# Im2col on one core: eight channels per partition and three uneven loads

## The chip, the cores and the metric

The kernel runs on one core of a Trainium2 chip. The metric is the device time of that core in microseconds (us); the time before is the median of three runs. One execution was also taken by the hardware profiler. Its span, from the first to the last instruction, is shorter than the time, because the time also holds what lies around the instructions. The engines named here are VectorE (DVE in the profile) and ScalarE (ACT), which copy; SyncE (SP), which issues the transfers; and the 16 DMA engines, which move data between the chip's main memory (HBM) and the on-chip memory of 128 partitions.

## The reference

The input `x` has the shape (16, 64, 32, 32) in float32, and `kernel_size` is 3. For each image and channel, the reference lays the 3 x 3 patches around all 30 x 30 positions side by side:

```python
cols = np.zeros((batch, c * kernel_size * kernel_size, h_out * w_out), dtype=np.float32)
for b in range(batch):
    col_idx = 0
    for i in range(h_out):
        for j in range(w_out):
            patch = x[b, :, i:i + kernel_size, j:j + kernel_size].copy()
            cols[b, :, col_idx] = patch.ravel()
            col_idx += 1
```

Read by output row, this is a plain copy: row (channel, ki, kj) of an image is the 30 x 30 window of that channel which starts at (ki, kj). Nothing is computed. One channel of 1,024 numbers (4,096 bytes) becomes nine windows of 900 numbers (32,400 bytes). In all 4.19 MB are read and 33.18 MB are written.

## The kernel before

Each partition holds two neighbouring channels (`CPP` = 2), so the 1,024 pairs of image and channel make four groups of 128 partitions. All four loads are issued first, each into a tile of its own. Then each group is copied window by window, in turn by ScalarE and VectorE, into one of two output tiles. The first group is stored one channel at a time, the other three whole.

```python
x_v = x.rearrange("b (cp c2) h w -> (b cp) c2 (h w)", c2=CPP)
out_v = out.rearrange("b (cp c2 kk) n -> (b cp) c2 (kk n)", c2=CPP, kk=KK)

in_pool = ctx.enter_context(tc.tile_pool(name="in_pool", bufs=n_groups))
out_pool = ctx.enter_context(tc.tile_pool(name="out_pool", bufs=2))

in_tiles = []
for g in range(n_groups):
    row0 = g * P
    in_tile = in_pool.tile([P, CPP, H, W], x.dtype, name="in_tile")
    nc.sync.dma_start(                                   # the loads
        out=in_tile,
        in_=x_v[row0 : row0 + P].rearrange("r c2 (h w) -> r c2 h w", h=H),
    )
    in_tiles.append(in_tile)

for g in range(n_groups):
    # ... row0, in_tile of this group
    out_tile = out_pool.tile([P, CPP, KK, HO, WO], x.dtype)
    ncopy = 0
    for c2 in range(CPP):
        for kk in range(KK):
            # ... src: the window in in_tile; dst: out_tile[:, c2, kk]
            if ncopy % 2 == 0:
                nc.scalar.copy(out=dst, in_=src)
            else:
                nc.vector.tensor_copy(out=dst, in_=src)
            ncopy += 1
        if g == 0:
            nc.sync.dma_start(                           # one channel
                out=out_v[row0 : row0 + P, c2],
                in_=out_tile[:, c2].rearrange("p kk i j -> p (kk i j)"),
            )
    if g != 0:
        nc.sync.dma_start(                               # two channels
            out=out_v[row0 : row0 + P].rearrange("r c2 n -> r (c2 n)"),
            in_=out_tile.rearrange("p c2 kk i j -> p (c2 kk i j)"),
        )
```

Of the kernel before, what the change touches and what calls it, by code (L numbers as in the profile page):

```python
# [1 line left out]

# [4 lines left out]


def _im2col_fast(ctx, tc, x, K, out, CPP):  # L10
    nc = tc.nc
    P = nc.NUM_PARTITIONS

    B, C, H, W = x.shape
    HO = H - K + 1
    WO = W - K + 1
    KK = K * K

    ROWS = B * C // CPP
    n_groups = ROWS // P  # L20

    x_v = x.rearrange("b (cp c2) h w -> (b cp) c2 (h w)", c2=CPP)
    out_v = out.rearrange("b (cp c2 kk) n -> (b cp) c2 (kk n)", c2=CPP, kk=KK)

    in_pool = ctx.enter_context(tc.tile_pool(name="in_pool", bufs=n_groups))
    out_pool = ctx.enter_context(tc.tile_pool(name="out_pool", bufs=2))

    in_tiles = []
    for g in range(n_groups):
        row0 = g * P  # L30
        in_tile = in_pool.tile([P, CPP, H, W], x.dtype, name="in_tile")
        nc.sync.dma_start(
            out=in_tile,
            in_=x_v[row0 : row0 + P].rearrange("r c2 (h w) -> r c2 h w", h=H),
        )
        in_tiles.append(in_tile)

    for g in range(n_groups):
        row0 = g * P
        in_tile = in_tiles[g]  # L40
        out_tile = out_pool.tile([P, CPP, KK, HO, WO], x.dtype)

        ncopy = 0
        for c2 in range(CPP):
            for kk in range(KK):
                ki, kj = divmod(kk, K)
                src = in_tile[:, c2, ki : ki + HO, kj : kj + WO]
                dst = out_tile[:, c2, kk]
                if ncopy % 2 == 0:
                    nc.scalar.copy(out=dst, in_=src)  # L50
                else:
                    nc.vector.tensor_copy(out=dst, in_=src)  # L52
                ncopy += 1

            if g == 0:
                nc.sync.dma_start(
                    out=out_v[row0 : row0 + P, c2],
                    in_=out_tile[:, c2].rearrange("p kk i j -> p (kk i j)"),
                )

        if g != 0:
            nc.sync.dma_start(
                out=out_v[row0 : row0 + P].rearrange("r c2 n -> r (c2 n)"),
                in_=out_tile.rearrange("p c2 kk i j -> p (c2 kk i j)"),
            )


def _im2col_generic(ctx, tc, x, K, out):
    nc = tc.nc
    P = nc.NUM_PARTITIONS  # L70

    B, C, H, W = x.shape
    HO = H - K + 1
    WO = W - K + 1
    KK = K * K

    x_rows = x.rearrange("b c h w -> (b c) (h w)")
    out_rows = out.rearrange("b ck n -> (b ck) n").rearrange(
        "(bc kk) n -> bc (kk n)", kk=KK
    )  # L80

    n_rows = B * C
    n_groups = (n_rows + P - 1) // P

    in_pool = ctx.enter_context(tc.tile_pool(name="in_pool", bufs=min(n_groups, 4)))
    out_pool = ctx.enter_context(tc.tile_pool(name="out_pool", bufs=2))

    for g in range(n_groups):
        row0 = g * P
        nrows = min(P, n_rows - row0)  # L90

        in_tile = in_pool.tile([P, H, W], x.dtype, name="in_tile_g")
        nc.sync.dma_start(
            out=in_tile[:nrows],
            in_=x_rows[row0 : row0 + nrows].rearrange("r (h w) -> r h w", h=H),
        )

        out_tile = out_pool.tile([P, KK, HO, WO], x.dtype, name="out_tile_g")
        for kk in range(KK):
            ki, kj = divmod(kk, K)  # L100
            src = in_tile[:nrows, ki : ki + HO, kj : kj + WO]
            dst = out_tile[:nrows, kk]
            if kk % 2 == 0:
                nc.scalar.copy(out=dst, in_=src)
            else:
                nc.vector.tensor_copy(out=dst, in_=src)

        nc.sync.dma_start(
            out=out_rows[row0 : row0 + nrows],
            in_=out_tile[:nrows].rearrange("p kk i j -> p (kk i j)"),  # L110
        )


@with_exitstack
def kernel(
    ctx: ExitStack,
    tc: tile.TileContext,
    x: bass.AP,
    kernel_size: bass.AP,
    out: bass.AP,  # L120
):
    nc = tc.nc
    P = nc.NUM_PARTITIONS

    K = int(kernel_size)
    B, C, H, W = x.shape
    HO = H - K + 1
    WO = W - K + 1
    KK = K * K
    assert out.shape == (B, C * K * K, HO * WO)  # L130

    dt_size = mybir.dt.size(x.dtype)

    CPP = 0
    for cand in (2, 1):
        if C % cand:
            continue
        rows = B * C // cand
        if rows % P:
            continue  # L140
        free_bytes = cand * KK * HO * WO * dt_size
        if free_bytes >= 2**16:
            continue
        n_groups = rows // P
        sbuf_need = 2 * free_bytes + n_groups * cand * H * W * dt_size
        if sbuf_need > 190 * 1024:
            continue
        CPP = cand
        break

    if CPP:
        _im2col_fast(ctx, tc, x, K, out, CPP)
    else:
        _im2col_generic(ctx, tc, x, K, out)


# [1 line left out]
_INS = ['x', 'kernel_size']  # L158
_OUTS = [((16, 576, 900), 'float32')]
#: Inputs that are plain numbers.  # L160
_NUMBERS = {'kernel_size': 3}


# [26 lines left out]
```

## Time and profile before

| | before |
|---|---|
| time, median of 3 runs | 92.78 us (92.61 to 93.19) |
| span of the profiled execution | 91.3 us |
| VectorE busy | 19.6 us, 36 copies, 623 ns each |
| ScalarE busy | 32.0 us, 36 copies, 938 ns each, and one table load |
| read from and written to HBM | 4.19 MB and 33.18 MB |

A copy's duration is longer than the step to the next copy on the same engine, since consecutive copies overlap a little; where the prediction adds up copies, it takes the step. The profile's page also gives the busy share of each engine and of the DMA in 40 equal slices of the span, each some 2.3 us, as digits in tenths. The span holds nine transfers of data: four loads and five stores, all issued by SyncE on one queue.

### The profile page before, as it was taken

The numbers are of one execution on the slowest core, as the hardware profiler recorded it, in microseconds if no ns is written. First come the engines' busy times: TensorE is split into PE (matmuls) and PEld (weight loads), VectorE is DVE, ScalarE is ACT, GpSimd is POOL, SyncE is SP. The second block draws the span as 40 slices with busy tenths as digits, with TensorE's granted clock in tenths as the row PEclk, the third lists the DMA queues.
The fourth block names the chain that finished last, engine by engine and source line by source line (L and its number), as shares of the span: only waits on it lengthen the run. The fifth ranks groups of instructions, "written<-read, shape, count | busy, mean of one in ns | idle before, by whom it ended". The sixth has DMA issues, their size and how long they took to land.

```text
span 91.3 us, 141 instructions
## 1 busy us (share of the span) xinstructions
DVE 19.6 (22%) x36; ACT 32.0 (35%) x37; POOL 0.2 (0%) x4
## 2 busy tenths in 40 slices
DVE  0059997000000049600000199000000000000000
ACT  5059999991000049980000199920000000000000
POOL 0000000000000000000000000000000000000000
DMA  2899999999999999899999999999999999999960
GB/s 36 373 406 431 427 463 426 412 440 440 426 426 440 554 454 398 369 426 398 454 454 454 454 454 454 454 454 454 454 454 426 426 398 398 426 426 426 426 284 0
DMA packets 1297, 37.37 MB, mean 409 GB/s; under 512 B 145, under 2 KB 145, under 8 KB 145
## 3 DMA queue, kind: packets, MB, share of 16 engines
q1 hardware_dynamic: 1296, 37.37, 95.7%
q14 instruction: 1, 0.00, 0.0%
HBM read 4.19 MB, written 33.18 MB: 409 GB/s over the span
## 4 chain that ended last, share of the span: by engine, by line
DMA 40%; ACT 24%; ACTq 1%; issue 0%
DMA out_dram<-out_tile 34%; ACT out_tile L50 24%; DMA in_tile<-in_x_dram 5%; ACTq L185 1%; ACTq L50 0%
## 5 line engine op out<-in xcount | busy, mean ns | idle before, releaser
L50 ACT COPY out_tile<-in_tile 128x900 f32<-128x900 f32 x36 | 30.7, 938 | 27.2 <-DMA out_dram<-out_tile 23.6
L52 DVE COPY out_tile<-in_tile 128x900 f32<-128x900 f32 x36 | 19.6, 623 | 37.6 <-DMA out_dram<-out_tile 31.9
L50 ACT ACT_TABLE_LOAD x1 | 1.3, 1283 | 0.7 <-PEq L171 0.7
L171 POOL MEMSET const-bfloat16-1.0<- 128x1 bf16 x1 | 0.1, 102 | 0.0
L171 POOL MEMSET const-uint8-127<- 128x1 uint8 x1 | 0.1, 102 | 0.0
L171 POOL MEMSET const-float32-0.0<- 128x1 f32 x1 | 0.1, 99 | 0.2 <-issue 0.2
L171 POOL MEMSET const-float32-1.0<- 128x1 f32 x1 | 0.1, 99 | 0.0
## 6 DMA issues: line engine op xcount, KB each, us to landing
out_dram<-out_tile SPq DMA_DIRECT2D x3, 8100.0 KB, 30.5
out_dram<-out_tile SPq DMA_DIRECT2D x2, 4050.0 KB, 16.6
in_tile<-in_x_dram SPq DMA_DIRECT2D x4, 1024.0 KB, 7.9
```

The lines of the kernel that those rows point to most:

```text
L50: nc.scalar.copy(out=dst, in_=src)
L52: nc.vector.tensor_copy(out=dst, in_=src)
L171: nc = _bacc.Bacc("TRN2", target_bir_lowering=False, num_devices=1)
L185: with _tile.TileContext(nc) as tc:
```

## The change

Each partition now holds eight neighbouring channels, so that the 1,024 pairs of image and channel fill the 128 partitions once. There is one input tile, which stays for the whole kernel, and it is filled by three loads: rows 0 to 31 of the partition's 256 rows (channel 0, 4 KB per partition), rows 32 to 239 (26 KB), rows 240 to 255 (2 KB). The channels are then copied in pairs into two output tiles that take turns as before. The first pair is stored one channel at a time, the other three pairs together. Of each five copies VectorE takes three and ScalarE two. The aim is to start copying after a small first load, to have few and long transfers after it, and to give the faster copy engine more of the copies. The generic path for other shapes and the choice of `CPP` are gone.

```diff
+    CPP = B * C // P
-    x_v = x.rearrange("b (cp c2) h w -> (b cp) c2 (h w)", c2=CPP)
+    x_v = x.rearrange("b (cp c2) h w -> (b cp) (c2 h w)", c2=CPP)
     out_v = out.rearrange("b (cp c2 kk) n -> (b cp) c2 (kk n)", c2=CPP, kk=KK)
-    in_pool = ctx.enter_context(tc.tile_pool(name="in_pool", bufs=n_groups))
+    in_pool = ctx.enter_context(tc.tile_pool(name="in_pool", bufs=1))
     out_pool = ctx.enter_context(tc.tile_pool(name="out_pool", bufs=2))
-    (the loop over four loads, each into a tile of its own)
+    in_tile = in_pool.tile([P, CPP, H, W], x.dtype, name="in_tile")
+    in_flat = in_tile.rearrange("p c h w -> p (c h w)")
+    cuts = [0, H, CPP * H - H // 2, CPP * H]
+    for r0, r1 in zip(cuts, cuts[1:]):
+        nc.sync.dma_start(
+            out=in_flat[:, r0 * W : r1 * W], in_=x_v[:, r0 * W : r1 * W]
+        )
+    on_act = (False, True, False, True, False)
+    n = 0
+    for c in range(0, CPP, 2):
+        out_tile = out_pool.tile([P, 2, KK, HO, WO], x.dtype, name="out_tile")
+        for s in range(2):
             for kk in range(KK):
                 ki, kj = divmod(kk, K)
-                src = in_tile[:, c2, ki : ki + HO, kj : kj + WO]
-                dst = out_tile[:, c2, kk]
-                if ncopy % 2 == 0:
+                src = in_tile[:, c + s, ki : ki + HO, kj : kj + WO]
+                dst = out_tile[:, s, kk]
+                if on_act[n % len(on_act)]:
                     nc.scalar.copy(out=dst, in_=src)
                 else:
                     nc.vector.tensor_copy(out=dst, in_=src)
-            if g == 0:
+            if c == 0:
                 nc.sync.dma_start(
-                    out=out_v[row0 : row0 + P, c2],
+                    out=out_v[:, s],
                     (from that half of out_tile, as before)
-        if g != 0:
+        if c > 0:
             nc.sync.dma_start(
-                out=out_v[row0 : row0 + P].rearrange("r c2 n -> r (c2 n)"),
+                out=out_v[:, c : c + 2].rearrange("p c n -> p (c n)"),
                 (from the whole out_tile, as before)
```

More of the change, by code (lines that the diff above doesn't have):

```diff
@@ L5, with _im2col @@
 import concourse.tile as tile
-from concourse import bass_utils, mybir
-from concourse._compat import with_exitstack
-def _im2col_fast(ctx, tc, x, K, out, CPP):
+from concourse import mybir
+def _im2col(ctx, tc, x, K, out):
     nc = tc.nc
@@ L17, in _im2col_fast @@
     KK = K * K
-    ROWS = B * C // CPP
-    n_groups = ROWS // P
-    x_v = x.rearrange("b (cp c2) h w -> (b cp) c2 (h w)", c2=CPP)
+    assert out.shape == (B, C * KK, HO * WO)
+    CPP = B * C // P
+    assert CPP * P == B * C and C % CPP == 0 and CPP % 4 == 0
+    x_v = x.rearrange("b (cp c2) h w -> (b cp) (c2 h w)", c2=CPP)
     out_v = out.rearrange("b (cp c2 kk) n -> (b cp) c2 (kk n)", c2=CPP, kk=KK)
-    in_pool = ctx.enter_context(tc.tile_pool(name="in_pool", bufs=n_groups))
+    in_pool = ctx.enter_context(tc.tile_pool(name="in_pool", bufs=1))
     out_pool = ctx.enter_context(tc.tile_pool(name="out_pool", bufs=2))
[L28 to L31, printed above, removed]
+    in_tile = in_pool.tile([P, CPP, H, W], x.dtype, name="in_tile")
+    in_flat = in_tile.rearrange("p c h w -> p (c h w)")
+    cuts = [0, H, CPP * H - H // 2, CPP * H]
+    for r0, r1 in zip(cuts, cuts[1:]):
         nc.sync.dma_start(
-            out=in_tile,
-            in_=x_v[row0 : row0 + P].rearrange("r c2 (h w) -> r c2 h w", h=H),
-        )
[L36 to L44, printed above, removed]
+            out=in_flat[:, r0 * W : r1 * W], in_=x_v[:, r0 * W : r1 * W]
+        )
+    on_act = (False, True, False, True, False)
[3 more added lines that the diff above has]
+        for s in range(2):
             for kk in range(KK):
                 ki, kj = divmod(kk, K)
-                src = in_tile[:, c2, ki : ki + HO, kj : kj + WO]
-                dst = out_tile[:, c2, kk]
-                if ncopy % 2 == 0:
+                src = in_tile[:, c + s, ki : ki + HO, kj : kj + WO]
+                dst = out_tile[:, s, kk]
+                if on_act[n % len(on_act)]:
                     nc.scalar.copy(out=dst, in_=src)
@@ L52, in _im2col_fast @@
                     nc.vector.tensor_copy(out=dst, in_=src)
-                ncopy += 1
-            if g == 0:
+                n += 1
+            if c == 0:
                 nc.sync.dma_start(
-                    out=out_v[row0 : row0 + P, c2],
-                    in_=out_tile[:, c2].rearrange("p kk i j -> p (kk i j)"),
+                    out=out_v[:, s],
+                    in_=out_tile[:, s].rearrange("p kk i j -> p (kk i j)"),
                 )
-        if g != 0:
+        if c > 0:
             nc.sync.dma_start(
-                out=out_v[row0 : row0 + P].rearrange("r c2 n -> r (c2 n)"),
-                in_=out_tile.rearrange("p c2 kk i j -> p (c2 kk i j)"),
-            )
[L68 to L114, printed above, removed]
+                out=out_v[:, c : c + 2].rearrange("p c n -> p (c n)"),
+                in_=out_tile.rearrange("p c kk i j -> p (c kk i j)"),
+            )
 def kernel(
-    ctx: ExitStack,
     tc: tile.TileContext,
@@ L121 @@
 ):
[L122 to L154, printed above, removed]
+    with ExitStack() as ctx:
+        _im2col(ctx, tc, x, int(kernel_size), out)
 _INS = ['x', 'kernel_size']
```

## The prediction, made before the changed kernel ran

> **What bounds the kernel now.** I read the page's busy row and slice rows first, because the two copy engines are so idle that something else must set the end:
>
> ```profile
> DVE 19.6 (22%) x36; ACT 32.0 (35%) x37; POOL 0.2 (0%) x4
> ...
> DMA  2899999999999999899999999999999999999960
> GB/s 36 373 406 431 427 463 426 412 440 440 426 426 440 554 454 398 369 426 398 454 454 454 454 454 454 454 454 454 454 454 426 426 398 398 426 426 426 426 284 0
> ...
> q1 hardware_dynamic: 1296, 37.37, 95.7%
> ```
>
> VectorE works for 22% of the span, ScalarE for 35%; the 16 DMA engines are full from the second slice (2.3 us) to the 38th (86.7 us), and the packets of the one data queue take 95.7% of 16 engines' span. There is no slice in between in which the DMA waits for a copy. A slice's rate jumps (369 to 554) because a packet of 64,800 bytes lasts as long as a slice; so I asked for longer stretches. Columns: stretch and length, busy time and count of each engine, PE clock, DMA share, GB/s:
>
> ```profile
> 3.00:11.00 8.00, 5.39 (x11) 5.39 (x7) 0.00 (x0) 1.00 1.01 426
> 14.00:30.00 16.00, 1.38 (x3) 6.89 (x9) 0.00 (x0) 1.00 1.00 433
> 33.10:52.13 19.03, 4.93 (x9) 7.69 (x9) 0.00 (x0) 1.00 1.01 436
> 52.13:71.10 18.97, 4.93 (x9) 7.69 (x9) 0.00 (x0) 1.00 1.01 437
> ```
>
> Loads run at 426 GB/s, one-channel stores at 433, two-channel stores at 436 and 437, with a DMA share of 1.0 in all four: the engines are full, and at nearly one rate in either direction.
>
> Then the DMA issues (count, size of each, median us from issue to landing) and the chain of waits in order of time:
>
> ```profile
> out_dram<-out_tile SPq DMA_DIRECT2D x3, 8100.0 KB, 30.5
> out_dram<-out_tile SPq DMA_DIRECT2D x2, 4050.0 KB, 16.6
> in_tile<-in_x_dram SPq DMA_DIRECT2D x4, 1024.0 KB, 7.9
> ```
> ```profile
> 0.73 4.85 DMA in_tile<-in_x_dram
> ...
> 20.92 31.21 DMA out_dram<-out_tile
> ...
> 52.23 0.95 ACT out_tile L50
> ```
>
> Asked one by one, the nine DMAs land in the order of their issue. The first load lands at 5.6, the fourth at 13.7 (11.6 after its issue at 2.1). The stores, issued at 10.0, 13.3, 20.9, 40.8 and 60.0, land at 23.4, 33.0, 52.1, 71.3 and 90.4. The gaps are 9.6 and 19.1 us, which are sizes and not waits. The chain's 24% of ScalarE is misleading: it goes back from the last store to the copies before it, although that store was issued at 60.0 and stood behind the fourth until 71.3. The 5 us chain piece at the start is real.
>
> The packet records close the account. There is one packet per partition and DMA, eight partitions per engine: 8,192 bytes take 309 ns, 32,400 take 1,200, 64,800 take 2,391 (medians). The last two give 27.2 bytes/ns and some 9 ns fixed per packet; 8,192 / 27.2 + 9 = 310 fits the first. Per engine: 4 x 8 x 309 + 2 x 8 x 1,200 + 3 x 8 x 2,391 ns = 9.9 + 19.2 + 57.4 = 86.5 us. The span is 91.3, so only 4.8 us are not packet time: 1.8 before the first packet starts, 0.9 after the last landing at 90.4, and about 2.1 of first-read delay, completion and unevenness of the engines. Of the last I can place one part: the fourth load's sixteen completions spread over 12.6 to 13.8, against 10.2 to 10.6 for the third, and some load packets between 11.2 and 12.9 take 320 to 650 ns instead of 309, where the first store's packets follow in the same rings. The slowest engine loses about 0.75 us there (13.75 instead of 10.55 + 2.47 = 13.0) and keeps that loss to the end.
>
> **What the Trainium skill says.** All from its page "DMA: Bandwidth & Descriptors". The section "Where 436 GB/s comes from" puts the fabric's ceiling at 435 GB/s; the trace agrees with 436 to 437 in the long stores. "Queues, rings and completion order" says that each DMA engine takes descriptors of a ring in order; the landings in order of issue fit. "Why small descriptors are slow (HBM only)" names a fixed overhead per packet; here it is some 9 ns. "Latency and other measured facts" has copies with a row pitch of 512 KiB at 207 GB/s against 214 in full, and at half of that only from 4 MiB. The new loads have a pitch of 32 KiB, far below, and the new stores one of 259,200 bytes, no power of two. No run here shows those pitches yet.
>
> **The change part by part.**
>
> Bytes: none added or removed. Stores are still two of one channel and three of two channels, with the same 32,400 and 64,800 bytes contiguous per partition: 76.6 us of packets per engine, unchanged.
>
> Loads: four packets of 8,192 per partition become 4,096, 26,624 and 2,048. By the fitted line these are 159, 987 and 84 ns; times 8 partitions 1.27 + 7.90 + 0.67 = 9.84 us against 9.89. Gain: 0.05 us. One issue on SyncE less (425 ns median), but the first starts the stream at the same 0.73, so nothing.
>
> The first wait: the first load is half as large, so it lands 8 x (309 - 159) = 1.2 us earlier, at about 4.4. Channel 0 is now 5 copies on VectorE (a start every 538 ns in the trace) and 4 on ScalarE (844 ns): 3 x 0.844 + 0.94 = 3.5 us. The first store is issued at about 7.9 rather than 10.0. That puts it in the rings earlier, but behind loads that run until about 12.4. Worth nothing by itself.
>
> What has to be tested is whether every later store is still issued before the one ahead of it has drained. Reckon about 1.0 us from issue to first packet (0.73 to 1.75 for the first load).
> - Store 1: issue 7.9, ready 8.9; loads drain 12.3. Slack 3.4.
> - Store 2: channel 1 must now wait for the 26 KB load, landing at 4.4 + 7.9 = 12.3, or 13 if the late loss falls on it. 6 copies on VectorE, 3 on ScalarE: 6 x 0.538 = 3.3. Issue 16.3, ready 17.3; store 1 drains at about 21.9. Slack 4.6.
> - Store 3: 18 copies, 11 on VectorE (5.9) and 7 on ScalarE (5.9). Issue 22.3, ready 23.3; store 2 drains at 31.5. Slack 8.
> - Store 4: its buffer comes free when store 2 lands, 33.0; 10 on VectorE, 8 on ScalarE, 6.8 us. Issue 39.9; store 3 drains at 50.6. Slack 10.
> - Store 5: buffer free at 52.1; 5.9 to 6.0 us. Issue 58.2; store 4 drains at 69.8. Slack 11.
>
> The new split of the copies (43 on VectorE, 29 on ScalarE, from 36 and 36) takes ScalarE's 7.7 us per tile to about 6: all of it beside transfers. So no store is late, and the sum is 92.78 - 0.05, within the scatter of the three runs (92.61 to 93.19).
>
> **The rivals.**
>
> 1. The first copies wait for all three loads, if the one input tile is released as a whole rather than by region. Then they start at about 13.4, store 1 is issued at 17 and its packets begin at 18, while the DMA has drained at 12.3: 5.7 us more, 98.5. Against it: separate cuts would have no sense then. For it: the kernel before, with four input tiles, shows no case. Chance 4%.
>
> 2. The strided layout slows the transfers. All stores and the large load now step over eight channels per partition instead of two. Before, the two one-channel stores already stepped (32,400 bytes at a pitch of 64,800) and ran at 433. A loss of 2% needs 1.9 us, over 2% of all packet time or 19% of load time. Chance 5%.
>
> 3. The turn from loads to stores goes differently. The 0.75 us lost there may vanish, since a small load ends the stream and the store stands ready 3.4 us ahead (some 92.0), or grow as much (93.5) because more store packets are ready beside small ones. Plausible either way, and both under 1%; this sets the width of my range.
>
> 4. A real gain over 2% would need transfers above 437 GB/s or fewer bytes. With 86.4 us of packets, 1.8 ahead and 0.9 behind, and 0.8 because the first packets last 1.04 to 1.25 us instead of 0.31, the floor of the span is 89.9 for sixteen even engines; with the 1.5 by which the time exceeds the span, 91.4. Chance 3%.
>
> **Range and chances.** I take 92.6: minus 0.05 for packets and minus a little for the turn. The range 92.0 to 93.4 holds the turn's gain below, and its loss and the scatter above. Faster by over 2% (under 90.9) 3%, within 2% 91%, slower by over 2% (over 94.6) 6%, which is most of rivals 1 and 2.
>
> **What would show it.** Right, if DMA is full from slice 2 to 38 again, the first store is issued near 8 and the second near 16, the five stores land 9.6 or 19.1 us apart with the last near 90.3, and ScalarE falls to about 28.5 us busy, VectorE rises to 27. Wrong, if copies start at 13 instead of 4.4 (rival 1), if a 64,800-byte store takes over 19.5 us between landings or the loads land after 14.5 (rival 2), or if an empty slice stands between two stores.

## The result and the profile after

The changed kernel takes 93.47 us (median of 4 runs, 93.40 to 93.60) against 92.69 us of the kernel before in its 4 runs: a ratio of 1.0077, with an interval of 1.0048 to 1.0106. (The ratios in this document are estimates with 95% intervals; they can differ a little from the quotient of the two medians, 1.0084 here.) It is slower by 0.8%, a difference that its runs show clearly. The time lies just above the range of the prediction (92.0 to 93.4), and within the 2% to which the prediction gave 91%. All later runs of the kernel before have a median span of 91.0 us and a time 1.8 us above it; the profile of before shown above (91.3) was one of its longer executions. The changed kernel's span is 91.7 in the profile.

The page of the changed kernel, first the engines' busy time, then the DMA's share in 40 slices and its rate, then the data queue:

```profile
DVE 23.5 (26%) x43; ACT 26.2 (29%) x30; POOL 0.2 (0%) x4
...
DMA  3999979999999999999999999999989799997990
GB/s 39 434 442 430 372 298 438 396 438 453 453 424 396 438 453 452 452 452 452 452 452 452 453 452 452 452 452 452 452 368 424 339 396 452 452 424 339 424 452 0
...
q1 hardware_dynamic: 1152, 37.37, 96.4%
```

As before, the DMA engines are the full ones and nothing waits for a copy: no slice before the last is empty. But the fifth and sixth slices (9.2 to 13.8 us), with the digits 9 and 7, move 372 and 298 GB/s, the least of the first half after the start.

In time, with the SyncE rows showing when transfers were issued (start, length, engine, line, what, how many):

```profile
4.58 3.48 ACT L49 COPY out_tile<-in_tile 128x900 f32<-128x900 f32 x4 [2.56 <-DMA in_tile<-in_x_dram]
4.58 2.78 DVE L51 COPY out_tile<-in_tile 128x900 f32<-128x900 f32 x5 [4.58 <-DMA in_tile<-in_x_dram]
8.08 9.09 SPq L54 DMA_DIRECT2D out_dram<-out_tile  x2
13.43 8.54 ACT L49 COPY out_tile<-in_tile 128x900 f32<-128x900 f32 x10 [5.38 <-DMA in_tile<-in_x_dram]
13.43 9.23 DVE L51 COPY out_tile<-in_tile 128x900 f32<-128x900 f32 x17 [6.08 <-DMA in_tile<-in_x_dram]
```

The copies do start at 4.6 and the first store is issued at 8.1, as predicted. Between 8.1 and 13.4 no copy runs at all; the engines wait for the 26 KB load, which was to land at 12.3 and lands at 13.4. The issues (count, size, median us to landing) have it too:

```profile
in_tile<-in_x_dram SPq DMA_DIRECT2D x1, 3328.0 KB, 12.2
in_tile<-in_x_dram SPq DMA_DIRECT2D x1, 512.0 KB, 3.8
in_tile<-in_x_dram SPq DMA_DIRECT2D x1, 256.0 KB, 12.4
```

Issued at 1.16 and 1.64, the last two land at 13.4 and 14.1. From there all is as before: the stores land at 23.8, 33.4, 52.6, 71.7 and 90.8, with gaps of 9.6 and three times 19.1. Against the profile of before (23.4 to 90.4) the whole difference of 0.4 us is there when the first store lands, and stays. (The medians differ by 0.8 us, more than the two profiles, because the profiled execution of before was 0.3 us longer than its median span.)

The place can be narrowed. The first line is the window from 10.5 to 13.5 us of the kernel before, the second the same window of the changed one (columns as in the prediction; the last two are DMA share and GB/s):

```profile
10.50:13.50 3.00, 3.00 (x7) 3.00 (x5) 0.00 (x0) 1.00 1.08 427
```
```profile
10.50:13.50 3.00, 0.07 (x1) 0.07 (x1) 0.00 (x0) 1.00 1.00 306
```

The share is full in both, the rate falls from 427 to 306 GB/s: the packets last longer. (A window counts a packet whole where it starts, so that a share can exceed 1; the rate over the share is 395 against 306.) In the packet records, the last 26 KB packet of each of the 16 engines, all begun between 10.7 and 11.1, takes 1.24 to 2.17 us, 1.68 on average, where 0.99 is the median. To compare kernels with loads of different sizes I use one number, the **stretch**: for all load packets on the loads' queue that end after 10.4 us, the duration less what the fitted line of the prediction gives for their size, summed and divided by 16 engines. It is 0.24 us for the kernel before and 0.89 us for the changed one. Each value of it, here and below, comes from the one profiled execution of that kernel.

### The profile page after: what moved, and what is told of

Same layout as the page of the kernel before. It is cut to its first block, busy times and chain, and to the rows that moved or that the text cites. A ratio compares the mean times of both kernels' runs of the same rounds, so it can differ in the third digit from the quotient of the medians.

```text
span 91.7 us, 138 instructions
## 1 busy us (share of the span) xinstructions
DVE 23.5 (26%) x43; ACT 26.2 (29%) x30; POOL 0.2 (0%) x4
## 4 chain that ended last, share of the span: by engine, by line
DMA 46%; DVE 16%; DVEq 1%; SPq 0%; issue 0%
DMA out_dram<-out_tile 33%; DVE out_tile L51 16%; DMA in_tile<-in_x_dram 13%; DVEq L102 1%; SPq L34 0%; DVEq L51 0%; SPq L59 0%
## 5 line engine op out<-in xcount | busy, mean ns | idle before, releaser
L49 ACT COPY out_tile<-in_tile 128x900 f32<-128x900 f32 x29 | 24.9, 940 | 31.8 <-DMA out_dram<-out_tile 23.8
L51 DVE COPY out_tile<-in_tile 128x900 f32<-128x900 f32 x43 | 23.5, 624 | 35.2 <-DMA out_dram<-out_tile 24.5
## 6 DMA issues: line engine op xcount, KB each, us to landing
in_tile<-in_x_dram SPq DMA_DIRECT2D x1, 256.0 KB, 12.4
```

## The experiments

Four theories fit this profile. **P**: the long packets are at fault; at the turn from loads to stores every engine has one of 26 KB in hand. **Q**: reading eight channels per partition, 32 KB apart, is slow. **T**: the short 2 KB packets are at fault. **S**: a store that is issued earlier and stands waiting while the loads still run stretches them. Times are medians of 4 to 22 runs, with one exception that is named, and ratios are to runs of the kernel before on the same chip.

### Other cuts of the loads, same layout

```diff
-    cuts = [0, H, CPP * H - H // 2, CPP * H]
+    cuts = [0, 2 * H, 4 * H, 6 * H, 8 * H]           # four even loads
+    cuts = [0, H, CPP * H]                           # two loads, 4 and 28 KB
+    cuts = [c * H for c in range(CPP + 1)]           # eight loads
```

Four even loads:

> Edit: the changed kernel with four loads of 8 KB per partition instead of 4, 26 and 2 KB. Theory P (the loss sits in the long load packets: the last 26 KB packet of every DMA engine lasted 1.68 us on average instead of 0.99): the loads end as in the kernel before, slowest completion of the last near 13.7 instead of 14.09, last store lands near 90.4 instead of 90.84, ratio to before 0.997 to 1.003. Theory Q (the loads read eight channels per partition, 32 KB apart, and that is slow): still 14.1 and 1.006 to 1.010. Theory S (a store that is ready two microseconds earlier disturbs the loads): the first store is issued at about 9.1 here, between 8.1 and 10.0, so a loss of about half.

Two loads:

> Edit: the changed kernel without the 2 KB load, loads of 4 and 28 KB per partition. Theory P: as the changed kernel or a little worse, last load complete near 14.1, ratio to before 1.006 to 1.011. Rival T (the 2 KB packets are what costs, being short reads at the turn to the stores): back to 13.7 and 0.997 to 1.003.

Eight loads:

> Edit: the changed kernel with eight loads of 4 KB per partition, one channel each; the first store is issued at about 8.1 as in the changed kernel. Theory P: the turn costs no more than before, perhaps 0.2 to 0.4 us less; 64 packets per engine of 159 ns make 10.2 us against 9.84; last load complete near 13.7, ratio 0.995 to 1.003. Theories Q and S: as the changed kernel, 1.006 to 1.010.

Measured: four loads of 8 KB 93.08 us, ratio 1.0039 (1.0024 to 1.0054), first store issued at 9.0, stretch 0.56. Two loads 93.47, 1.0078 (1.0062 to 1.0093), issue 7.8, stretch 1.19. Eight loads 93.45, 1.0076 (1.0061 to 1.0091), issue 7.8, stretch 0.79. The eight loads refute P: packets of 4 KB are as slow at the end as one of 26. The two loads refute T: without the 2 KB packets nothing is better. The four even loads lie half way, as S had it; their ratio is above what P and below what Q expected, but its interval reaches into P's range and the last store lands at 90.4, as P had it, so that this kernel alone would not part P from S.

### No store behind the loads

```diff
-    for c in range(0, CPP, 2):
+    for c in range(CPP - 2, -1, -2):
-        for s in range(2):
+        for s in (1, 0):
             ...
-            if c == 0:                 # the pair stored one channel at a time
+            if c == CPP - 2:
             ...
-        if c > 0:
+        if c < CPP - 2:
```

> Edit: the changed kernel with the channels taken from the last to the first, so that the first copies need all three loads and no store is queued while loads run. It will be about 5 us slower; only the landing of the loads matters. If 26 KB reads end slowly by themselves, the 26 KB load completes at 12.5 to 13.4 and the 2 KB load at 13.3 to 14.1 as in the changed kernel, the last 26 KB packets lasting some 1.7 us. If the loss comes from the store queued behind (its packets sharing the engine with the last load packets), the last long packets last about 1.0 us and the last load completes by 13.2.

The first copies wait for the late loads, so the first store is issued at 16.8. (Three copies of channel 7 start between 12.4 and 12.9, before the 2 KB load with that channel's last 16 rows has landed at 13.0: this kernel leaves out the wait for it, and its output is not right there. The transfers are all there.) The time is 97.5 us, one run. Its load issues, to be held against those of the changed kernel above:

```profile
in_tile<-in_x_dram SPq DMA_DIRECT2D x1, 3328.0 KB, 11.2
in_tile<-in_x_dram SPq DMA_DIRECT2D x1, 512.0 KB, 3.7
in_tile<-in_x_dram SPq DMA_DIRECT2D x1, 256.0 KB, 11.4
```

The same three loads with the same packets land one microsecond sooner, at 12.4 and 13.0, and the stretch is 0.00. So the loads' last packets are not slow by themselves, be it for size or layout. What slows them in the changed kernel is then something that this kernel lacks at that time, first of all the waiting store. (One smaller loss does belong to these loads: between 5 and 10.4 us the packets exceed the fitted line by 0.21 us per engine in the changed kernel, but by 0.11 here too, with no store behind them, and by none in the kernel before. Its cause stays open.)

### The first store earlier or later

If that is so, the loss should follow the time at which the first store is issued. In the changed kernel this can be moved with nothing else by giving ScalarE, the slower copier, more of channel 0's nine copies:

```diff
-                if on_act[n % len(on_act)]:
+                if (c + s == 0 and "101101101"[kk] == "1") or (c + s > 0 and on_act[n % len(on_act)]):
```

The string gives ScalarE six of the nine; two other kernels had "111101111", eight, and all nine.

> Edit: the changed kernel, but of channel 0's nine copies ScalarE takes six and VectorE three, so that the first store is issued near 9.8 instead of 8.1; loads, layout and everything after are the same. Theory S (the earlier the first store stands queued behind the loads, the more the last load packets are stretched): the mean stretch per DMA engine falls from some 840 ns to about 250, the last load completes by 13.6, ratio to before 0.999 to 1.003. Theory Q (eight channels per partition make the reads slow): unchanged, 1.006 to 1.010.

> Edit: the same with eight of channel 0's copies on ScalarE, first store issued near 11.4, its packets ready near 12.4 when the loads are about to end. Theory S: hardly any stretch (under 100 ns), last load complete by 13.1, ratio 0.993 to 0.998, faster than both kernels. Theory Q: 1.006 to 1.010. If the stretch comes from the turn itself and not from how long the store has been queued, it stays where it is in the run with the issue at 9.8.

> Edit: the same with all nine of channel 0's copies on ScalarE, first store issued near 12.3 and its packets ready near 13.3, after the loads have ended. Theory S: no stretch at all, loads end at 13.0 as in the run with the loads alone, but the DMA engines stand idle for about 0.3 to 1 us; ratio 0.996 to 1.003. Theory Q: over 1.006.

In the kernel before, the first store can be brought forward the same way, by cutting its first load in two and taking the new split of the copies:

```diff
+        for c2s in (((0, 1), (1, 2)) if g == 0 else ((0, 2),)):
             nc.sync.dma_start(       # channels c2s[0] to c2s[1] of in_tile
-                if ncopy % 2 == 0:
+                if ncopy % 5 in (1, 3):
```

> Edit: the kernel before (two channels per partition, loads of at most 8 KB per partition) with the first load cut into its two channels and the 3 to 2 split of the copies, so that its first store is issued near 8.0. Theory S: it loses what the changed kernel loses, mean stretch 600 to 1000 ns, ratio 1.005 to 1.009. Theories P (long load packets) and Q (eight-channel layout): as before, 0.998 to 1.002.

And it can be held back, by giving ScalarE seven of the first nine copies:

```diff
-                if ncopy % 2 == 0:
+                if ("110111011"[ncopy] == "1") if g == 0 and c2 == 0 else ncopy % 2 == 0:
```

> Edit: the kernel before, but of its first channel's nine copies ScalarE takes seven, so that the first store is issued near 11.6 instead of 10.0; nothing else. Theory S (a store queued early behind the loads stretches the last load packets): the stretch of some 240 ns per engine goes, last load complete near 13.0, ratio to before 0.993 to 0.998. If the effect belongs to the eight-channel kernel alone: 0.999 to 1.002.

Last, the changed kernel with its own split of the copies, but two loads of 16 KB, so that the first data comes late:

```diff
-    cuts = [0, H, CPP * H - H // 2, CPP * H]
+    cuts = [0, 4 * H, 8 * H]
```

> Edit: the changed kernel with two loads of 16 KB per partition; the split of the copies stays as in the changed kernel. The first load lands near 8.1, so the first store is issued near 11.6 because its data comes late, not because ScalarE copies it. Theory S: as in the run with the issue at 11.3, ratio to before 0.993 to 0.998, first store lands near 22.6. If that run's gain came from the split of the copies: 1.005 to 1.010.

In order of the issue:

| kernel | first store issued, us | stretch, us | last load complete, us | ratio to before (interval) |
|---|---|---|---|---|
| changed, as it is | 8.1 | 0.89 | 14.1 | 1.0077 (1.0048 to 1.0106) |
| before, store early | 8.1 | 0.75 | 14.6 | 1.0150 (1.0128 to 1.0171) |
| changed, four even loads | 9.0 | 0.56 | 13.5 | 1.0039 (1.0024 to 1.0054) |
| changed, six copies on ScalarE | 9.7 | 0.35 | 13.4 | 0.9991 (0.9983 to 1.0000) |
| before, as it is | 10.0 | 0.24 | 13.8 | 1 |
| changed, eight copies on ScalarE | 11.3 | 0.00 | 13.0 | 0.9947 (0.9928 to 0.9966) |
| changed, two loads of 16 KB | 11.6 | 0.00 | 13.0 | 0.9958 (0.9943 to 0.9973) |
| before, store late | 11.7 | 0.00 | 13.1 | 0.9960 (0.9946 to 0.9974) |
| changed, nine copies on ScalarE | 12.4 | 0.00 | 13.2 | 1.0005 (0.9992 to 1.0017) |

In this table the order of the stretches is the order of the issues, for both layouts, for load packets of 8, 16 and 26 KB, and for either way of moving the issue. (The two kernels with an issue at 7.8, above, had 0.79 with packets of 4 KB and 1.19 with 28 KB; so the size of the load packets may count in the second place.) Theory Q falls with the two kernels of the old layout. The second row missed its expectation in size (1.005 to 1.009), and its ratio does not measure the store's effect alone. Averaged over the engines, its last load completes at 13.99, 0.84 us later than in the kernel before (13.15). Half of that, 0.41 us, is already there when the load ahead of it completes (10.78 against 10.37), and most of this half when the cut first load does (5.73 against 5.40). Only the other half comes at the end, where the stretch is 0.75 against 0.24. Besides, 2.0 us of its time lie outside the span, instead of 1.8. Why stays open in both.

The fastest kernel is the changed one with eight of the first copies on ScalarE: 92.35 us (92.23 to 92.64), faster than both, though the three best rows have overlapping intervals. Its timeline and its window of 10.5 to 13.5 us:

```profile
4.40 6.84 ACT L49 COPY out_tile<-in_tile 128x900 f32<-128x900 f32 x8 [2.40 <-DMA in_tile<-in_x_dram]
4.40 0.63 DVE L51 COPY out_tile<-in_tile 128x900 f32<-128x900 f32 x1 [4.40 <-DMA in_tile<-in_x_dram]
11.27 4.82 SPq L54 DMA_DIRECT2D out_dram<-out_tile  x2
...
12.36 9.23 DVE L51 COPY out_tile<-in_tile 128x900 f32<-128x900 f32 x17 [7.32 <-DMA in_tile<-in_x_dram]
```
```profile
10.50:13.50 3.00, 1.15 (x3) 1.89 (x3) 0.00 (x0) 1.00 1.01 424
```

One VectorE copy and a VectorE that then idles for 7.3 us, in the fastest kernel of all: the store comes 3.2 us later than in the changed kernel, and the rate of the turn is 424 GB/s again instead of 306. The kernel before with the late store has it too, with both copy engines at work all the time:

```profile
10.50:13.50 3.00, 3.00 (x7) 3.00 (x5) 0.00 (x0) 1.00 1.02 432
```

So copies running beside the loads are not what stretches them. GB/s alone would mislead in other kernels, as the same window shows of the eight loads of 4 KB and of the two loads of 16 KB:

```profile
10.50:13.50 3.00, 3.00 (x7) 3.00 (x4) 0.00 (x0) 1.00 1.26 417
10.50:13.50 3.00, 3.00 (x6) 3.00 (x5) 0.00 (x0) 1.00 0.91 391
```

The first has the higher rate and a stretch of 0.79, the second none. The rate over the share tells them apart: 331 against 430 GB/s.

The last row of the table is the other edge: issued at 12.4, the store's first packet begins at 13.2, while the loads' last packet ended at 12.8; what the stretch no longer costs, idle engines do.

### What about the waiting store matters

Two more kernels asked for the mechanism. In one the first store goes through ScalarE's DMA queue and so does not stand in the rings of the loads; in the other it is cut into three, so that its packets are a third as long.

```diff
-                nc.sync.dma_start(
+                (nc.scalar if s == 0 else nc.sync).dma_start(
```

> Edit: the changed kernel with its first store, still issued near 8.1, on ScalarE's DMA queue; the loads and all other stores stay on SyncE's. If the loss needs the store to stand in the same rings behind the loads, it goes: second store lands near 32.9 or earlier, ratio to before 0.994 to 1.001. If it comes from load and store packets being at work together on an engine, the longer mixing makes it larger: ratio 1.008 to 1.020.

```diff
+                for k0 in (6, 3, 0) if s == 0 else (0,):
+                    k1 = k0 + 3 if s == 0 else KK
                     nc.sync.dma_start(       # windows k0 to k1 of this channel
```

> Edit: the changed kernel with its first store cut into three of three windows each (10,800 bytes per partition and packet), all issued from about 8.1 on. If what stretches the loads is the size of the store packets that stand next in the ring, the stretch falls to about a third, ratio to before 0.998 to 1.003; if only how long a store has been queued counts, the stretch stays near 840 ns, ratio 1.006 to 1.010.

On the other queue: 93.39 us, ratio 1.0069 (1.0054 to 1.0085), stretch 1.01 us. Neither expectation is met; the loss is neither gone nor larger. The issues of that kernel:

```profile
out_dram<-out_tile ACTq DMA_DIRECT2D x1, 4050.0 KB, 18.1
...
in_tile<-in_x_dram SPq DMA_DIRECT2D x1, 3328.0 KB, 13.4
in_tile<-in_x_dram SPq DMA_DIRECT2D x1, 512.0 KB, 3.7
in_tile<-in_x_dram SPq DMA_DIRECT2D x1, 256.0 KB, 21.9
```

The 2 KB load now lands only at 23.6, since its packets take turns with the store's (they begin evenly spread from 12.5 to 23.1). That much fits the Trainium skill ("DMA: Bandwidth & Descriptors", section "Queues, rings and completion order"), which says that a DMA engine goes round the queues it has work for, packet by packet. But the store, issued at 7.9, has its first packet in the records at 12.4 only, when the first of the last 26 KB packets ends, and not between the 26 KB packets, none of which begins after 11.5; turns after each recorded packet do not explain that. It stretches the loads while no packet of it is recorded.

In thirds: 93.79 us, ratio 1.0108 (1.0093 to 1.0123), just above what was expected if only the waiting counts (1.006 to 1.010), stretch 0.97. A third of the size does not lessen the stretch; some 0.14 us of the added time are the packets themselves (24 x 406 ns against 8 x 1,200 ns).

So it is not the size of the store's packets, nor that they share a ring with the loads. How a store that waits lengthens the read packets ahead of it stays open. Neither a waiting store of a few bytes nor a waiting transfer of another kind was tried; that a waiting load does not do it can be read in the kernel before, whose fourth load waits from 2.1 on while the packets of the second and third keep to their 309 ns.

## Why the prediction was wrong

**The step that failed** is in the part on the first wait: the first store "in the rings earlier, but behind loads that run until about 12.4. Worth nothing by itself." It was worth a loss. Being ready 3.4 us ahead was entered as slack, as if a waiting store were free; each microsecond by which the store was issued before some 11.3 cost about 0.2 to 0.3 us of the loads' last two microseconds (0.24 at 10.0, 0.56 at 9.0, 0.89 at 8.1).

**The term that was mis-sized** is rival 3. I had seen the loss at the turn in the profile of before, 0.75 us on the slowest engine, and had placed it where the first store follows. But I took its sign to be open, and even gave the early store as the reason why it might vanish. The loads with nothing behind them complete at 13.0, as the sum of packets had it (4.4 + 7.9 + 0.7); with the store of the changed kernel behind them, at 14.1. So the term is 1.1 us there. "Grow as much (93.5)" was the branch that came, and the range ended at 93.4. Of the listed signs only the last landing showed it, at 90.8 instead of near 90.3; that of loads landing after 14.5 was set for rival 2, and they landed by 14.1.

**What was right.** The DMA's packet time bounds both kernels. The sum of packets held: one packet per partition at 27.2 bytes/ns and 9 ns, medians of 159, 987 and 84 ns for the new loads as computed. The stores' gaps of 9.6 and 19.1 us did not change with the new pitch (rival 2), and the first copies did not wait for all loads (rival 1). The issues of the stores, predicted at 7.9, 16.3, 22.3, 39.9 and 58.2, came at 8.1, 16.8, 22.7, 40.4 and 58.8; none was late, and the new split of the copies was hidden.

**Two smaller errors.** The busy time of the copy engines was summed from durations that overlap (28.5 and 27 us against 26.2 and 23.5 in the profile). And the 1.5 us added to the span to get the time came from one long execution; all later runs of before give 1.8. With that, the floor of rival 4 would have been 91.7; the best kernel stands at 92.35.

## What to carry to other kernels

Where the DMA engines are the bound, a full share in the slices is not full rate: compare GB/s over the share in the same window, and look there at the turn from loads to stores. An earlier store is not free when it must wait behind loads anyway; here the best issues (11.3 to 11.7) were 0.9 to 1.4 us before the loads' last packet ended, about the time from such an issue to its first packet (0.8 to 1.0 us), and both earlier (9.7) and later (12.4) were slower. A delay that leaves a copy engine idle for seven microseconds was worth 1.3% over the kernel as it was changed (ratios to before of 0.9947 against 1.0077).

## What the runs showed of the hardware

A store that has been issued but has no packet at work lengthened load packets on all 16 DMA engines (the last 26 KB packets of the changed kernel to between 1.24 and 2.17 us, instead of 0.99), and in sum the more the earlier it was issued (0.24 us per engine at 10.0, 0.89 at 8.1); on a queue of its own it did the same (stretch 1.01 us), and its packets still began only at 12.4 us, 4.5 us after the issue. The store packets themselves keep their time to within 6% in all kernels.
